# Mixer weights split by DMA on GpSimd's queue, and all convolution taps on VectorE, in a hybrid decoder trunk

## Chip, core and metric

One of the cores of a Trainium2 chip runs the whole program. The metric is the device time of one execution in microseconds (us); the median of three runs of the kernel before is 1012.71 us.

## What is computed

Two layers, each a half-step SwiGLU FFN, a token mixer and a second half-step FFN, all with RMSNorm before and after, on 256 tokens of 1024 channels in float32. The mixer, cut to what matters here:

```python
def hybrid_mixer(h, w_in, ..., w_out):
    p = h @ w_in                      # 1024 x 2064
    gq, gk, gv, gr, glr, ca, cg, sq, sk, sv = jnp.split(p, offsets, axis=-1)
    o_gla  = gla_group(...)           # gated linear attention, 4 heads
    o_conv = conv_group(ca, cg, ...)  # GLU, causal depthwise convolution of width 31, LayerNorm, swish
    o_swa  = swa_group(sq, sk, sv, swa_sinks)   # sliding-window attention, 8 query heads
    return jnp.concatenate([o_gla, o_conv, o_swa], axis=-1) @ w_out   # 1024 x 1024
```

## The kernel before

**Tiling.** The 256 tokens are two tiles of 128 (t = 0 and 1). Every large product is made of three matmuls (`mm3`, lines 178 to 181): activations and weights are each split into a rounded part (`hi`, type float32r) and the rest (`lo`), and hi·hi, hi·lo and lo·hi are added up in PSUM.

**The weight stream.** All weights come as units, in the order of use, through `emit_unit` (line 148). A unit is up to 512 KB: 128 partitions by 1024 floats. A unit of kind "f" belongs to an FFN, one of kind "m" to a mixer. For every unit SyncE's queue (SP) issues a load into one of four `raw` buffers (line 155), ScalarE (ACT) rounds it into `hi` (line 159), and VectorE (DVE) subtracts to get `lo` (line 165); in a mixer 10 of the 28 units take GpSimd (POOL) for that subtraction. There are eight `hi` and eight `lo` buffers, called slots here. A unit takes the slot of the unit eight before it, when TensorE (PE) has read that one for the last time. The raw load needs only a raw buffer, so it runs ahead of the slot.

**The mixer's units.** In this text m0 to m27 are the units of one mixer. The input projection has five groups of columns in the order c, k, q, b, a (line 116), with four units each: m0 to m3 (c), m4 to m7 (k, half as wide), m8 to m11 (q), m12 to m15 (b), m16 to m19 (a). m20 to m27 are the output projection. `c0` is group c for tile 0. The order in which the mixer's pieces are written stands in `SCRIPT` (line 120): c0 k0 c1 T016 k1 q0 S00 S01 ... where T016 is 16 convolution taps, S the attention scores, O attention outputs, G, K, L and P the linear attention, Y the LayerNorm, W the output projection. The framework then orders the instructions of each engine, and each engine takes its own queue in that order; an instruction that waits holds all behind it on its engine, DMA issues included.

**Between FFN and mixer.** `post` (line 276) adds the FFN's output to x and `pre` (line 253) makes the normalized, transposed input of the mixer, for each tile. Both need `rstd`, a power on POOL (line 243): four of them at the start of a mixer, for post and pre of tiles 0 and 1.

**Convolution.** 31 taps for two halves of the channels (c = 0, 1). For c = 0 DVE multiplies and adds (line 636); for c = 1 ACT multiplies (line 639) and POOL adds (line 640). Tap 0 of both is ACT's.

Of the kernel before, what the change touches and what calls it, by code (L numbers as in the profile page):

```python
# [7 lines left out]
F32 = mybir.dt.float32  # L8
# [3 lines left out]
AF = mybir.ActivationFunctionType  # L12
ALU = mybir.AluOpType
# [3 lines left out]
P = 128  # L17
# [25 lines left out]
def trunk_kernel(  # L43
# [6 lines left out]
    V, G, A, PE = nc.vector, nc.gpsimd, nc.scalar, nc.tensor  # L50

    cp = ctx.enter_context(tc.tile_pool(name="cp", bufs=1))
    wp = ctx.enter_context(tc.tile_pool(name="wp", bufs=1))
# [7 lines left out]
    def nm(s):  # L61
        uid[0] += 1
        return f"{s}_{uid[0]}"
# [1 line left out]
    def ps_tile(tag):  # L65
        return pa.tile([P, 512], F32, tag=tag, name=nm(tag), bufs=2)

# [1 line left out]
    A.preload_act_table_set("silu_and_others")  # L69
    xs = []  # L70
    for t in range(T):
# [7 lines left out]
    A.dma_start(out=grow, in_=norm_g.rearrange("l n (k p) -> (l n k) p", p=P))  # L79
    ident = cst[:, C_ID:C_ID + P]  # L80

# [1 line left out]
    units = []  # L83

    DSPLIT = 2
# [57 lines left out]
    NB = 8  # L143
    RAW = 4
    split = {}
    state = {"emitted": 0, "released": 0, "m": 0}

    def emit_unit(i):
        src, nk, w, kind = units[i]
        raw = wp.tile([P, 1024], F32, tag="raw", name=nm("raw"), bufs=RAW)  # L150
        hi = wp.tile([P, 1024], F32R, tag="hi", name=nm("hi"), bufs=NB)
        lo = wp.tile([P, 1024], F32R, tag="lo", name=nm("lo"), bufs=NB)
        n = nk * w
        rv = raw[:, :n].rearrange("p (k n) -> p k n", k=nk)
        nc.sync.dma_start(out=rv, in_=src)
        if i == 1:
            for t in range(1, T):
                nc.sync.dma_start(out=xs[t], in_=x_d[t * P:(t + 1) * P, :])
        A.copy(out=hi[:, :n], in_=raw[:, :n])  # L159
        eng = V  # L160
        if kind == "m":
            state["m"] += 1
            if (state["m"] - 1) % 28 >= 8 and state["m"] % 2 != 0:
                eng = G
        eng.tensor_tensor(out=lo[:, :n], in0=raw[:, :n], in1=hi[:, :n].bitcast(F32), op=ALU.subtract)  # L165
        split[i] = (hi[:, :n].rearrange("p (k n) -> p k n", k=nk),
                    lo[:, :n].rearrange("p (k n) -> p k n", k=nk))

    def top_up():
        while state["emitted"] < len(units) and state["emitted"] - state["released"] < NB:  # L170
            emit_unit(state["emitted"])
            state["emitted"] += 1
# [62 lines left out]
        nc.sync.dma_start(out=g, in_=norm_g[l, n].partition_broadcast(P))  # L235
        return g

# [1 line left out]
    def rstd_of(ss, m=1.0):  # L239
        r = sp.tile([P, 1], F32, tag="rstd", name=nm("rstd"), bufs=8)  # L240
        v = sp.tile([P, 1], F32, tag="var", name=nm("var"), bufs=2)
        V.tensor_scalar(out=v, in0=ss[:, 0:1], scalar1=ss[:, 1:2], scalar2=m * RMS_EPS, op0=ALU.add, op1=ALU.add)  # L242
        G.tensor_tensor(out=r, in0=v, in1=mhalf[:, 0:1], op=ALU.pow)  # L243
        return r
# [39 lines left out]
            xh = xs[t][:, h * 512:(h + 1) * 512]  # L284
            V.scalar_tensor_tensor(out=xh, in0=ys[h], scalar=r, in1=xh, op0=ALU.mult, op1=ALU.add)

# [1 line left out]
    def ffn(first, xT, after, setup=None):  # L288
        acc = [[None, None] for _ in range(T)]
        for t in range(T):  # L290
# [104 lines left out]
                x0 = after(t, acc[t])  # L395
        return [x0, lambda: after(1, acc[1])]

# [1 line left out]
    def sigm(out, in_, scale):  # L399
        A.activation(out=out, in_=in_, func=AF.Exp, scale=scale)  # L400
        A.activation(out=out, in_=out, func=AF.Ln, bias=one)
        A.activation(out=out, in_=out, func=AF.Exp, scale=-1.0)

    def mixer(l, first, xT, after):
        with tc.issue_after(state["silu"].ins):
            ld = A.preload_act_table_set("natural_log_exp_and_others")
        with tc.issue_after(ld.ins):
            return mixer_body(l, first, xT, after)

    def mixer_body(l, first, xT, after):  # L410
# [39 lines left out]
        def tmp(ring, w=256, parts=P):  # L450
            r = mp.tile([P, 256], F32, tag=f"t{ring}", name=nm(f"t{ring}"), bufs={"c": 3, "g": 5, "s": 3}[ring])
            return r[:parts, :w]
# [3 lines left out]
        glr = [mp.tile([P, 16], F32, tag=f"glr{t}", name=nm("glr")) for t in range(T)]  # L456
        qk = [mp.tile([P, 256], F32, tag=f"qk{t}", name=nm("qk")) for t in range(T)]

        # convolution: GLU
        def conv_in(t, ps):  # L460
            sg = tmp("c")
            sigm(sg, ps[:, 256:512], nr[t])
            u = tmp("c")
            V.scalar_tensor_tensor(out=u, in0=ps[:, 0:256], scalar=xT[t][2], in1=sg, op0=ALU.mult, op1=ALU.mult)
            pt = ps_tile("tr")
            for c in range(2):
                PE.transpose(out=pt[:, c * P:(c + 1) * P], in_=u[:, c * P:(c + 1) * P], identity=ident)
            o0 = TAPS - 1 + t * P
            A.copy(out=upad[:, :, o0:o0 + P], in_=pt[:, :256].rearrange("p (c n) -> p c n", c=2))
# [15 lines left out]
            A.activation(out=qk[t], in_=ps[:, 0:256], func=AF.Copy, scale=r)  # L485
            A.activation(out=v_[t][:, 0:136], in_=ps[:, 256:392], func=AF.Copy, scale=r)

        # GLA: log gates, their sums inside a chunk, decayed keys and queries
        kx = mp.tile([P, 2, P], F32, tag="kx", name=nm("kx"))

        REG = []
# [130 lines left out]
            V.tensor_tensor(out=og, in0=og, in1=gr[t], op=ALU.mult)  # L622
            return og

        # convolution: taps, LayerNorm, swish
        yt = sp.tile([P, 512], F32, tag="junk", name=nm("cy"), bufs=1)
        y = [yt[:, 0:S], yt[:, S:2 * S]]
        taps = []

        def tap(c, k):  # L630
            w = cwT[:, l, c, :]
            yc, uk = y[c], upad[:, c, k:k + S]
            if k == 0:
                A.activation(out=yc, in_=uk, func=AF.Identity, scale=w[:, 0:1], bias=w[:, TAPS:TAPS + 1])
            elif c == 0:
                V.scalar_tensor_tensor(out=yc, in0=uk, scalar=w[:, k:k + 1], in1=yc, op0=ALU.mult, op1=ALU.add)  # L636
            else:
                m = tmp("c")
                A.activation(out=m, in_=uk, func=AF.Copy, scale=w[:, k:k + 1])  # L639
                G.tensor_tensor(out=yc, in0=m, in1=yc, op=ALU.add)  # L640

        for k in range(TAPS):
            for c in range(2):
                taps.append(lambda c=c, k=k: tap(c, k))
# [24 lines left out]
            V.tensor_tensor(out=yn, in0=yn, in1=sy, op=ALU.mult)  # L669
            return yn  # L670

        # sliding-window attention
        sv = [mp.tile([P, P], F32, tag=f"sv{t}", name=nm("sv")) for t in range(T)]

        def kv_in(t, ps):
# [88 lines left out]
        scs, qps, gates, qs, ats, ogs, yns = {}, {}, {}, {}, {}, {}, {}  # L764
# [43 lines left out]
            run(op)  # L808
        return [x0[0], lambda: after(1, accs[1])]

# [1 line left out]
    late = []  # L812
    xT = [pre(0, 0, 0), lambda: pre(1, 0, 0)]
    top_up()
# [70 lines left out]
```

## Time and profile before

| | us |
|---|---|
| runs | 1016.26, 1011.55, 1012.71 (median 1012.71) |
| span of the profiled execution | 1010.4 |
| PE busy | 967.4 (96% of the span) |
| DVE busy | 620.7 (61%) |
| ACT busy | 544.3 (54%) |
| POOL busy | 138.8 (14%) |
| DMA, mean over the span | 169 GB/s, 171.26 MB |

The median lies 2.3 us above the span of the profiled execution; this is what lies around the instructions, and the spread of runs (4.7 us). The two mixers take some 128 us each, from about 196 to 324 us and from about 700 to 832 us; the rest is FFN. A profile's slices show PE full in the FFNs; in the mixers the busy shares of DVE and POOL rise and that of PE falls. Busy time of PE is that of pipelined matmuls, so the start times of successive matmuls are used below rather than their durations.

### The profile page before, as it was taken

What the parts mean: (1) busy time and instruction counts of PE and PEld (TensorE: products, weight loads), DVE (VectorE), ACT (ScalarE), POOL (GpSimd) and SP (SyncE); (2) the same over time, 40 slices, a digit from 0 to 9 for tenths busy, and PEclk for the clock granted to TensorE, in tenths of its full rate; (3) what the DMA queues carried; (4) which work ended last, traced back from release to release, by engine and by line L of the source; (5) the groups of instructions that cost most, each with busy time, mean ns of one, the idle gap of its engine ahead of it and who ended that gap; (6) DMA issues with size and microseconds to landing.
All of it is one profiled execution on the core that took longest, in us unless ns stands there. A gap on an engine that the chain in (4) does not pass through costs nothing.

```text
span 1010.4 us, 13066 instructions
## 1 busy us (share of the span) xinstructions
PE 967.4 (96%) x4721; PEld 823.0 (81%) x4721; DVE 620.7 (61%) x948; ACT 544.3 (54%) x927; POOL 138.8 (14%) x154
## 2 busy tenths in 40 slices
PE   7999999997889999999999999999878999999997
PEld 7788888876678988888898888898666898888896
DVE  6555455569898755454576455456698885555453
ACT  7534444577775744444475444356877585444441
POOL 1120000037541000000000000001675210000000
PEclk9999999999999999999999999999989999999999
DMA  8756655553233766655567666464422348666541
GB/s 284 263 178 197 187 167 179 147 186 119 77 89 121 242 200 198 187 171 169 151 197 253 191 182 193 148 224 144 129 84 85 96 157 268 190 186 194 158 148 42
DMA packets 81953, 171.26 MB, mean 169 GB/s; under 512 B 6178, under 2 KB 29920, under 8 KB 81889
## 3 DMA queue, kind: packets, MB, share of 16 engines
q1 hardware_dynamic: 79952, 168.97, 53.8%
q10 hardware_dynamic: 1937, 1.45, 0.8%
q8 instruction: 37, 0.61, 0.2%
q14 instruction: 27, 0.22, 0.1%
HBM read 169.36 MB, written 1.05 MB: 169 GB/s over the span
## 4 chain that ended last, share of the span: by engine, by line
PE 82%; DVE 9%; DMA 3%; ACT 3%; issue 2%; POOL 1%; SPq 0%; POOLq 0%; DVEq 0%; ACTq 0%
PE gu L180 17%; PE gu L179 17%; PE gu L181 17%; PE ga L179 4%; PE ga L180 4%; PE ga L181 4%; PE sa L181 4%; PE sa L179 4%; PE sa L180 4%; DVE cy L636 3%; PE tr L319 2%; DVE E L520 1%; DVE lo L165 1%; PE sa L709 1%; PE tr L262 1%
## 5 line engine op out<-in xcount | busy, mean ns | idle before, releaser
L165 DVE TENSOR_TENSOR lo<-raw,hi 128x1024 fp32r<-128x1024 f32 (+3 forms) x316 | 370.2, 1177 | 317.3 <-ACT hi L159 316.8
L159 ACT CAST hi<-raw 128x1024 fp32r<-128x1024 f32 (+2 forms) x336 | 332.1, 995 | 363.8 <-PE gu L181 218.8
L179 PE MATMUL gu<-hi,xh 128*128 128x512 f32 (+2 forms) x864 | 326.2, 378 | 0.9 <-ACT xh L266 0.9
L180 PE MATMUL gu<-lo,xh 128*128 128x512 f32 (+2 forms) x864 | 325.3, 376 | 0.0
L181 PE MATMUL gu<-hi,xl 128*128 128x512 f32 (+2 forms) x864 | 325.0, 376 | 0.0
L181 PEld LDWEIGHTS gu<-hi,xl 128*128 128x128 f32 x864 | 163.6, 189 | 23.0
L180 PEld LDWEIGHTS gu<-lo,xh 128*128 128x128 f32 x864 | 163.8, 190 | 22.6 <-DVE lo L165 0.4
L179 PEld LDWEIGHTS gu<-hi,xh 128*128 128x128 f32 x864 | 163.5, 189 | 23.0 <-ACT xh L266 1.3
L243 POOL TENSOR_TENSOR rstd<-var,mhalf 128x1 f32<-128x1 f32 x24 | 13.2, 549 | 732.2 <-DVE var L242 732.2
L181 PE MATMUL sa<-hi,hl 128*128 128x512 f32 x176 | 69.0, 392 | 0.0
L179 PE MATMUL ga<-hi,hh 128*128 128x512 f32 x176 | 68.8, 391 | 0.0
L179 PE MATMUL sa<-hi,hh 128*128 128x512 f32 x176 | 68.8, 391 | 0.0
L181 PE MATMUL ga<-hi,hl 128*128 128x512 f32 x176 | 68.6, 390 | 0.0
L180 PE MATMUL ga<-lo,hh 128*128 128x512 f32 x176 | 68.6, 390 | 0.0
L180 PE MATMUL sa<-lo,hh 128*128 128x512 f32 x176 | 68.5, 389 | 0.0
L165 POOL TENSOR_TENSOR lo<-raw,hi 128x1024 fp32r<-128x1024 f32 (+1 forms) x20 | 49.0, 2457 | 31.2 <-ACT hi L159 31.2
L640 POOL TENSOR_TENSOR cy<-tc,cy 128x256 f32<-128x256 f32 x60 | 48.4, 806 | 31.4 <-ACT tc L639 27.8
L636 DVE SCALAR_TENSOR_TENSOR cy<-upad,cwT,cy 128x256 f32<-128x256 f32 x60 | 43.6, 726 | 1.3
L181 PEld LDWEIGHTS ga<-hi,hl 128*128 128x128 f32 x176 | 33.0, 188 | 6.9
L180 PEld LDWEIGHTS sa<-lo,hh 128*128 128x128 f32 x176 | 33.1, 188 | 6.9
L181 PEld LDWEIGHTS sa<-hi,hl 128*128 128x128 f32 x176 | 33.0, 188 | 6.8
L179 PEld LDWEIGHTS sa<-hi,hh 128*128 128x128 f32 x176 | 33.0, 188 | 6.8
(182 smaller groups left out, 1009.9 us busy)
## 6 DMA issues: line engine op xcount, KB each, us to landing
raw<-in_ffn_w_down_dram SPq DMA_DIRECT2D x88, 512.0 KB, 3.4
raw<-in_ffn_w_gate_dram SPq DMA_DIRECT2D x64, 512.0 KB, 3.8
raw<-in_ffn_w_up_dram SPq DMA_DIRECT2D x64, 512.0 KB, 3.8
raw<-in_ffn_w_gate_dram SPq DMA_DIRECT2D x32, 384.0 KB, 3.3
raw<-in_ffn_w_up_dram SPq DMA_DIRECT2D x32, 384.0 KB, 3.4
raw<-in_w_in_dram SPq DMA_DIRECT2D x16, 512.0 KB, 5.5
raw<-in_w_out_dram SPq DMA_DIRECT2D x16, 512.0 KB, 3.4
raw<-in_w_in_dram SPq DMA_DIRECT2D x16, 392.0 KB, 3.7
```

The costliest lines, as they stand in the source:

```text
L159: A.copy(out=hi[:, :n], in_=raw[:, :n])
L165: eng.tensor_tensor(out=lo[:, :n], in0=raw[:, :n], in1=hi[:, :n].bitcast(F32), op=ALU.subtract)
L179: PE.matmul(out=out, lhsT=xh, rhs=wh, start=start, stop=False)
L180: PE.matmul(out=out, lhsT=xh, rhs=wl, start=False, stop=False)
L181: PE.matmul(out=out, lhsT=xl, rhs=wh, start=False, stop=stop)
L243: G.tensor_tensor(out=r, in0=v, in1=mhalf[:, 0:1], op=ALU.pow)
L262: PE.transpose(out=ps[:, i * P:(i + 1) * P], in_=x[:, k * P:(k + 1) * P], identity=ident)
L319: PE.transpose(out=ps[:, i * P:(i + 1) * P], in_=h[:, i * P:(i + 1) * P], identity=ident)
L520: V.tensor_tensor(out=E[:, o:o + P // 4 * R].rearrange("p (c n) -> p c n", n=n), in0=bv[:, :, n - 1:n].to_broadcast([P, P // (4 * s_), n]) ...
L636: V.scalar_tensor_tensor(out=yc, in0=uk, scalar=w[:, k:k + 1], in1=yc, op0=ALU.mult, op1=ALU.add)
L640: G.tensor_tensor(out=yc, in0=m, in1=yc, op=ALU.add)
L709: PE.matmul(out=pqv, lhsT=qp[:, g * 2 + pi, :], rhs=kbd[:, g, :, 0:W], start=True, stop=True)
```

## The change

For units of kind "m" there is no raw buffer and no load on SP any more. GpSimd's queue issues a DMA from the weights straight into `hi`, which converts float32 to float32r; ACT writes `lo` = -`hi`; then GpSimd's queue issues a second DMA that reads the same weights again and adds them into `lo`. No subtraction is left for a mixer's units on DVE or POOL. In the convolution the taps of c = 1 go to DVE as well, so ACT's multiplications and POOL's additions are gone.

```diff
 def emit_unit(i):
     src, nk, w, kind = units[i]
-    raw = wp.tile([P, 1024], F32, tag="raw", name=nm("raw"), bufs=RAW)
     hi = wp.tile(...)
     lo = wp.tile(...)
     n = nk * w
+    split[i] = (hi view, lo view)
+    if kind == "m":
+        G.dma_start(out=split[i][0], in_=src)
+        A.activation(out=lo[:, :n], in_=hi[:, :n].bitcast(F32), func=AF.Copy, scale=-1.0)
+        G.dma_start(out=split[i][1], in_=src, accum_op=ALU.add)
+        return
+    raw = wp.tile([P, 1024], F32, tag="raw", name=nm("raw"), bufs=RAW)
...
     A.copy(out=hi[:, :n], in_=raw[:, :n])
-    eng = V
-    if kind == "m":
-        state["m"] += 1
-        if (state["m"] - 1) % 28 >= 8 and state["m"] % 2 != 0:
-            eng = G
-    eng.tensor_tensor(out=lo[:, :n], in0=raw[:, :n], in1=hi[:, :n].bitcast(F32), op=ALU.subtract)
+    V.tensor_tensor(out=lo[:, :n], in0=raw[:, :n], in1=hi[:, :n].bitcast(F32), op=ALU.subtract)
...
     if k == 0:
         A.activation(out=yc, in_=uk, func=AF.Identity, scale=w[:, 0:1], bias=w[:, TAPS:TAPS + 1])
-    elif c == 0:
+    else:
         V.scalar_tensor_tensor(out=yc, in0=uk, scalar=w[:, k:k + 1], in1=yc, op0=ALU.mult, op1=ALU.add)
-    else:
-        m = tmp("c")
-        A.activation(out=m, in_=uk, func=AF.Copy, scale=w[:, k:k + 1])
-        G.tensor_tensor(out=yc, in0=m, in1=yc, op=ALU.add)
```

The order on the engines moves with it. In the next two fences stands POOL's queue where the first mixer begins: L243 is the power for `rstd`, in the order post and pre of tile 0, post and pre of tile 1, and L421 a small step for pre's. Before:

```order
L243 TENSOR_TENSOR rstd_1664<-var_1665,mhalf 128x1
L243 TENSOR_TENSOR rstd_1679<-var_1680,mhalf 128x1
L421 TENSOR_SCALAR nr_1794<-rstd_1679 128x1
L243 TENSOR_TENSOR rstd_1846<-var_1847,mhalf 128x1
L243 TENSOR_TENSOR rstd_1861<-var_1862,mhalf 128x1
L421 TENSOR_SCALAR nr_1907<-rstd_1861 128x1
L165 TENSOR_TENSOR lo_1961<-raw_1959,hi_1960 128x1024
```

And of the change, in two pieces (hi_1567, hi_1584 and hi_1605 are m0 to m2; between the pieces stand the issues for the `hi` of m3 and m4, the power for pre of tile 0 and its L421; hi_1762, hi_1767 and hi_1772 are m5 to m7, and lo_1735, lo_1740, lo_1763, lo_1768 and lo_1773 the `lo` of m3 to m7):

```order
L156 DMA hi_1567<-in_w_in_dram 128x2x512
L156 DMA hi_1584<-in_w_in_dram 128x2x512
L158 DMA lo_1568<-in_w_in_dram 128x2x512
L156 DMA hi_1605<-in_w_in_dram 128x2x512
L158 DMA lo_1585<-in_w_in_dram 128x2x512
L158 DMA lo_1606<-in_w_in_dram 128x2x512
L243 TENSOR_TENSOR rstd_1661<-var_1662,mhalf 128x1
```

```order
L156 DMA hi_1762<-in_w_in_dram 128x2x256
L158 DMA lo_1735<-in_w_in_dram 128x2x512
L158 DMA lo_1740<-in_w_in_dram 128x2x256
L156 DMA hi_1767<-in_w_in_dram 128x2x256
L158 DMA lo_1763<-in_w_in_dram 128x2x256
L156 DMA hi_1772<-in_w_in_dram 128x2x256
L243 TENSOR_TENSOR rstd_1838<-var_1839,mhalf 128x1
L158 DMA lo_1768<-in_w_in_dram 128x2x256
L243 TENSOR_TENSOR rstd_1853<-var_1854,mhalf 128x1
L421 TENSOR_SCALAR nr_1899<-rstd_1853 128x1
L158 DMA lo_1773<-in_w_in_dram 128x2x256
```

Before, no other instruction stood between the powers; now the first stands behind the three DMA pairs of m0 to m2, and the last two stand between the pairs of m3 to m7.

The second place is DVE's queue where the convolution's taps (L636) meet the first attention scores (L713 before, L709 in the change). Before:

```order
L464 SCALAR_TENSOR_TENSOR tc_1913<-gu_1816,rstd_1679,tc_1909 128x256
L165 TENSOR_TENSOR lo_1973<-raw_1971,hi_1972 128x1024
L165 TENSOR_TENSOR lo_1997<-raw_1995,hi_1996 128x1024
L165 TENSOR_TENSOR lo_2062<-raw_2060,hi_2061 128x784
L464 SCALAR_TENSOR_TENSOR tc_2005<-gu_1952,rstd_1861,tc_2001 128x256
L165 TENSOR_TENSOR lo_2086<-raw_2084,hi_2085 128x784
L636 SCALAR_TENSOR_TENSOR cy_1813<-upad,cwT,cy_1813 128x256 x13
L713 ISA sc_2132,mx_2133<-sa_2134,alibi,snk 128x128
```

And of the change:

```order
L270 SCALAR_TENSOR_TENSOR xl_1872<-tr_1886,gT,xh_1864 128x128
L464 SCALAR_TENSOR_TENSOR tc_1905<-gu_1808,rstd_1676,tc_1901 128x256
L464 SCALAR_TENSOR_TENSOR tc_1993<-gu_1944,rstd_1853,tc_1989 128x256
L636 SCALAR_TENSOR_TENSOR cy_1805<-upad,cwT,cy_1805 128x256 x33
L709 ISA sc_2102,mx_2103<-sa_2104,alibi,snk 128x128
```

The four subtractions of mixer units are gone from there, and 33 taps instead of 13 stand ahead of the first scores.

## Rows read from the trace of the kernel before

**Rows 1.** Busy time by engine, whole span: us, share, instructions
```profile
PE 967.4 (96%) x4721; PEld 823.0 (81%) x4721; DVE 620.7 (61%) x948; ACT 544.3 (54%) x927; POOL 138.8 (14%) x154
```

**Rows 2.** Busy time by stretch: both mixers, then a part of the first
```profile
core 0: us, PE busy (x) PEld busy (x) DVE busy (x) ACT busy (x) POOL busy (x), PEclk, DMA share, GB/s
196.00:324.00 128.00, 114.48 (x605) 94.15 (x604) 105.63 (x244) 91.96 (x228) 60.22 (x62) 0.97 0.34 109
700.00:832.00 132.00, 117.70 (x635) 99.60 (x634) 107.40 (x246) 94.51 (x228) 59.51 (x61) 0.96 0.37 120
244.00:300.00 56.00, 50.03 (x267) 41.09 (x265) 50.56 (x137) 43.00 (x114) 30.84 (x33) 0.95 0.27 86
```

**Rows 3.** Timeline of PE, first mixer: start, us, what, [idle before, releaser]
```profile
203.73 0.39 PE L179 MATMUL gu<-hi,xh 128*128 128x512 f32 x1
203.96 0.39 PE L180 MATMUL gu<-lo,xh 128*128 128x512 f32 x1
...
221.70 0.28 PE L181 MATMUL ga<-hi,xl 128*128 128x256 f32 x1
...
241.70 0.67 PE L709 MATMUL sa<-kbd,qp 128*128 128x256 f32 x2 [3.55 <-DVE mx L713]
...
244.04 0.63 PE L181 MATMUL gu<-hi,xl 128*128 128x512 f32 x1
```

**Rows 4.** Busy time by stretch, around the stall at 241.70
```profile
237.90:241.70 3.80, 0.25 (x2) 0.03 (x1) 3.73 (x8) 1.81 (x4) 3.74 (x3) 1.00 0.01 2
241.70:246.40 4.70, 4.70 (x15) 4.16 (x16) 4.70 (x18) 1.99 (x9) 3.91 (x4) 0.64 0.68 218
```

**Rows 5.** Groups of DVE by line, 196 to 324 us: xcount, busy us, mean ns
```profile
L636 DVE SCALAR_TENSOR_TENSOR cy<-upad,cwT,cy 128x256 f32<-128x256 f32 x30 | 22.1, 735 | 0.7
L165 DVE TENSOR_TENSOR lo<-raw,hi 128x1024 fp32r<-128x1024 f32 x7 | 11.9, 1700 | 5.3 <-ACT hi L159 5.3
L165 DVE TENSOR_TENSOR lo<-raw,hi 128x784 fp32r<-128x784 f32 x4 | 4.9, 1221 | 3.2 <-ACT hi L159 3.2
L165 DVE TENSOR_TENSOR lo<-raw,hi 128x512 fp32r<-128x512 f32 x4 | 2.5, 684 | 0.0
```

**Rows 6.** Timeline of DVE: taps beside POOL's additions, and one with POOL idle
```profile
228.79 12.22 DVE L636 SCALAR_TENSOR_TENSOR cy<-upad,cwT,cy 128x256 f32<-128x256 f32 x13
...
246.22 0.48 DVE L636 SCALAR_TENSOR_TENSOR cy<-upad,cwT,cy 128x256 f32<-128x256 f32 x1
```

**Rows 7.** Timeline of ACT: roundings of m0 to m3, sums of squares
```profile
183.57 1.05 ACT L159 CAST hi<-raw 128x1024 fp32r<-128x1024 f32 x1 [1.03 <-PE gu L181]
...
188.43 1.05 ACT L159 CAST hi<-raw 128x1024 fp32r<-128x1024 f32 x1 [0.94 <-PE sa L181]
...
195.97 0.60 ACT L250 ACTIVATE junk<-ga 128x512 f32<-128x512 f32 x1 [1.41 <-PE ga L181]
...
197.27 1.06 ACT L159 CAST hi<-raw 128x1024 fp32r<-128x1024 f32 x1 [0.61 <-PE sa L181]
```

**Rows 8.** Timeline of POOL: powers of post, tiles 0 and 1
```profile
196.99 0.57 POOL L243 TENSOR_TENSOR rstd<-var,mhalf 128x1 f32<-128x1 f32 x1 [140.36 <-DVE var L242]
...
205.72 0.57 POOL L243 TENSOR_TENSOR rstd<-var,mhalf 128x1 f32<-128x1 f32 x1 [4.38 <-DVE var L242]
```

**Rows 9.** DMA issues: KB each, median us from issue to landing
```profile
raw<-in_w_in_dram SPq DMA_DIRECT2D x16, 512.0 KB, 5.5
raw<-in_w_out_dram SPq DMA_DIRECT2D x16, 512.0 KB, 3.4
```

**Rows 10.** Groups of POOL and ACT by line, 196 to 324 us
```profile
L640 POOL TENSOR_TENSOR cy<-tc,cy 128x256 f32<-128x256 f32 x30 | 24.3, 809 | 15.5 <-ACT tc L639 13.7
L165 POOL TENSOR_TENSOR lo<-raw,hi 128x1024 fp32r<-128x1024 f32 (+1 forms) x10 | 24.5, 2454 | 15.2 <-ACT hi L159 15.1
L639 ACT ACTIVATE tc<-upad,cwT 128x256 f32<-128x256 f32 x30 | 14.1, 505 | 1.8 <-POOL cy L640 1.6
```

More of the change, by code (lines that the diff above doesn't have):

```diff
@@ L145, in trunk_kernel @@
     split = {}
-    state = {"emitted": 0, "released": 0, "m": 0}
+    state = {"emitted": 0, "released": 0}
     def emit_unit(i):
         src, nk, w, kind = units[i]
-        raw = wp.tile([P, 1024], F32, tag="raw", name=nm("raw"), bufs=RAW)
         hi = wp.tile([P, 1024], F32R, tag="hi", name=nm("hi"), bufs=NB)
@@ L153, in emit_unit @@
         n = nk * w
+        split[i] = (hi[:, :n].rearrange("p (k n) -> p k n", k=nk),
+                    lo[:, :n].rearrange("p (k n) -> p k n", k=nk))
+        if kind == "m":
[4 more added lines that the diff above has]
+        raw = wp.tile([P, 1024], F32, tag="raw", name=nm("raw"), bufs=RAW)
         rv = raw[:, :n].rearrange("p (k n) -> p k n", k=nk)
@@ L159, in emit_unit @@
         A.copy(out=hi[:, :n], in_=raw[:, :n])
-        eng = V
-        if kind == "m":
-            state["m"] += 1
-            if (state["m"] - 1) % 28 >= 8 and state["m"] % 2 != 0:
-                eng = G
-        eng.tensor_tensor(out=lo[:, :n], in0=raw[:, :n], in1=hi[:, :n].bitcast(F32), op=ALU.subtract)
-        split[i] = (hi[:, :n].rearrange("p (k n) -> p k n", k=nk),
-                    lo[:, :n].rearrange("p (k n) -> p k n", k=nk))
+        V.tensor_tensor(out=lo[:, :n], in0=raw[:, :n], in1=hi[:, :n].bitcast(F32), op=ALU.subtract)
     def top_up():
```

## The prediction

> **What bounds the kernel now.** I read the shares by engine first, then the two mixers as stretches of their own, then the places in them where PE waits, and last the times at which slots and sums come free.
>
> PE is busy 967.4 of 1010.4 us [rows 1], so what is left to win lies in the 43 us in which it is idle. The two mixers hold 13.5 (128 - 114.48) and 14.3 (132 - 117.70) of these, and in them the granted clock is 0.97 and 0.96 [rows 2], which costs about 3% of 128 and 4% of 132, 3.8 and 5.3 us. So a change that touches the mixers alone can win at most 13.5 + 14.3 + 3.8 + 5.3 = 37 us. From 244 to 300 us the idle time and the clock make 6.0 + 2.5 = 8.5 us, while DVE is busy 50.56 of 56 [rows 2]: there DVE sets the pace. The longest stall is of that kind: at 241.70 PE has waited 3.55 us for the first scores [rows 3], which stand behind 13 taps on DVE. In the stall PE was nearly idle; behind it 4.70 us ran at a mean granted clock of 0.64, below the upper level of 2.4 GHz, before the clock was full again [rows 4]. A stall thus costs about (1 - 0.64) x 4.70 = 1.7 us more than its length. Weights are not what PE waits for there: SP loads them into raw buffers ahead of the slot, and a slot that comes free needs only ACT's 1.05 us [rows 7] and the subtraction.
>
> **What the change takes off the engines.** In the first mixer DVE loses 11.9 + 4.9 + 2.5 = 19.3 us of subtractions [rows 5]. It gains 30 taps. A tap takes 0.48 us with POOL idle, but 13 of them took 12.22 us beside POOL's additions, 0.94 each [rows 6]; with these gone I price all 60 at 0.48, 28.8 us against 22.1 now [rows 5], +6.7. DVE is relieved by 12.6 us a mixer. POOL loses 24.3 + 24.5 us of work, ACT 14.1 us of multiplications [rows 10]; neither bounds the mixer, so I cost both at nothing. ACT's rounding of a unit becomes a negation of the same size. The second reading of the weights adds 2 x 28 units, some 25 MB; the DMA share in a mixer is 0.34 to 0.37 [rows 2], so bandwidth covers that and I cost it at nothing; were the queue full, it would show in the landing time below.
>
> **What it adds: two landings in a row.** The raw load ran ahead of the slot. The first DMA now writes the slot itself, so it can't be issued before PE has let go of it; then come a landing, 1.05 us of ACT and a second landing. No DMA of POOL's queue and none that adds is in the trace. The nearest rows are the unit loads on SP, 3.4 us from issue to landing for the output projection and 5.5 for the input projection [rows 9]. I take 5.5 for both, since it is the load of the same matrix at the same place, and keep 3.4 for both as the lower end and 11 for the adding one (twice 5.5, since it reads two things) as the upper. For POOL's time to issue I take 0.5 us.
>
> By 5.5 us the page "DMA: Bandwidth & Descriptors" of the Trainium skill disagrees: its fit for this path ("Anatomy of one DMA") is 2.0 us plus the bytes by 436 GB/s, so 3.2 us for 524288 bytes, an estimate by that page, and no run here shows it. By that figure the sum would be that of the rival below that wins.
>
> **Step by step, first mixer.** m0's slot is free at 183.5, m2's at 188.4 [rows 7]. In POOL's queue m2's first issue stands behind m0's second, which waits for landing (189.0) and ACT (190.1): m2 lands at 196.1 and is negated by 197.2. ACT's sums of squares for post of tile 0 stand behind that negation; the last half began at 195.97 [rows 7], now both run from 197.2 to 198.4. The power, 196.99 before [rows 8], starts at 198.7: +1.7 us for all that follows.
>
> m3's slot is free at 197.3 [rows 7]. Its first issue is behind that power, 199.3; landed 204.8, second issue 205.9, landed 211.4. Group c starts at 203.73 + 1.7 = 205.4 and has used m0 to m2 by 209.2 (a matmul each 0.23 us [rows 3]): PE waits 2.2 us. m5 to m7 get their slots at 204.1 to 205.4. POOL's queue now takes turns, and each second issue waits for the landing before it: m5 at 204.1 and 210.3, m6 at 207.6 and 213.8, m7 at 210.8 and 217. m7 is whole at 222.5. The power for post of tile 1, 205.72 before [rows 8], comes at 211.3, +5.6, and that for pre at 215.5; both are early enough for c1, which stands behind m7. Behind it come five half-wide matmuls of k0 (half of 0.23 each, 0.6), 19 of c1 (4.4) and 24 half-wide ones of k1 (2.8), so with 1.7 for the slow clock k1 ends at about 222.5 + 0.6 + 4.4 + 2.8 + 1.7 = 232.0, against 222.0 [rows 3]: PE loses about 10 us.
>
> Group q goes into the slots that c1 lets go, from 221.5 to about 229. By the same count its last unit lands at 246.2, and q1 ends at 248.5 instead of 244.4 [rows 3]: only 4.1 us later, since PE was waiting for DVE in that stretch. Meanwhile DVE does its 33 taps, 33 x 0.48 = 15.8 us, from about 231 to 247: the taps are off the path. The first three units of b keep PE until about 252; m15 is whole at 255.7 (3.7 us of waiting), and m16, which follows 1.1 us of b0, at 259.9 (3.1 us). Attention's scores fill some of these 6.8 us; I take 5.5. So a0 is 4.1 + 5.5 = 9.6 us late.
>
> **The sum.** Per mixer: 9.6 us until a0, plus 1.7 for the slow clock behind the last of these waits, less what DVE's relief wins back. Of the 8.5 us between 244 and 300 I give back half, 4.2, because those stalls are also waits on attention's own chain. That is +7.1 a mixer, +14.2 for both: 1010.4 + 14.2 = 1024.6 for the span, and with the 2.3 us by which the median stands above it **1027 us**. What the FFNs do is unchanged.
>
> **Rivals.**
>
> *The relief decides (faster).* If both DMAs land in 3.4 us, each of the eight landings in a row on the way to a0 is 2.1 us shorter, 17 us, more than the 9.6: weights no longer bind, DVE's 12.6 us relief is on the path, and the whole 8.5 us is won in each mixer, 1012.7 - 17 = 996. It decides once a landing costs about 4.3 us or less (9.6 / 8 = 1.2 less than 5.5). For it speaks the 3.4 of the output projection and DVE's share; against it the 5.5 at the very place, and the powers behind DMAs.
>
> *The adding DMA is slow.* At 11 us its five landings in a row (m2, m7, m11, m19 and the output projection's last) add 5 x 5.5 = 27.5 us a mixer: 1027 + 55 = 1082. For it: it reads, adds and writes; against it: nothing in the trace.
>
> *DVE holds POOL's DMAs up.* The taps were slowed from 0.48 to 0.94 us beside POOL [rows 6], so the two engines do get in each other's way. If a run of 33 taps kept POOL from issuing, m11's first issue, due at about 234, would wait until 247, 12.6 us in each mixer: 1027 + 25 = 1052. The page "SBUF — State Buffer" of the Trainium skill ("SBUF: two separate sides") has such a rule: GpSimd can't write descriptors while VectorE runs in a two-port mode. It names copies, casts and `tensor_scalar` for that, and infers that two SBUF inputs alone don't do it, so by that page the taps would not.
>
> *No difference.* The waits for weights and the relief cancel: 1012.7. For it: q1 loses only 4.1 of the 10 us.
>
> That the conversion doesn't round would change `lo`, not the time.
>
> **How the numbers follow.** Chances: the forecast's case (about 1015 to 1045) 0.46, relief 0.22, slow adding DMA 0.16, held up 0.06, no difference 0.10. The likeliest is the forecast, so 1027 stands. Its own range is 1015 to 1045. To leave out no more than 2 in 10 the range goes down to the relief's 996 and up into the slow case, where 7.5 us for the adding DMA instead of 11 gives 1027 + 2 x 5 x 2 = 1047 and 10 us 1072: 996 to 1072. A measurement of this kernel tells 0.5%, 5 us, from no change. Faster by more than that: 0.23 (relief, and a little of no difference); within it 0.11; slower 0.66.
>
> **What would show it.** Right: in the first 30 us of each mixer PE waits for `lo` and `hi` of m3, m7 and m11; the power for post of tile 1 starts some 5 us later after the FFN's last matmul; taps take 0.48 us; the stretch from the first scores to the mixer's end is shorter than now. Wrong: PE waits that stay with DVE (then landings are short and it is faster), second issues that land more than 8 us after they go out, or gaps between POOL's issues just while DVE's taps run.

## The result, and the profile after

The changed kernel takes **1062.47 us** (1059.25 to 1065.36, 4 runs) against 1013.23 (1011.55 to 1016.26) for the kernel before on the same chip: ratio 1.0482, 95% interval 1.0462 to 1.0502. That is 49 us slower. The forecast was 14 us slower, so the sign was right and the size far off: 1062 lies above the forecast's own range, 1015 to 1045, and inside the wide one, 996 to 1072, only by the case of the slow adding DMA. The FFNs did not change; each mixer lost some 24.7 us.

The page's busy times and DMA queues, after [rows 1 for before]:

```profile
PE 988.1 (93%) x4721; PEld 838.2 (79%) x4721; DVE 567.5 (54%) x972; ACT 518.2 (49%) x867; POOL 144.5 (14%) x186
...
q1 hardware_dynamic: 66768, 143.67, 44.2%
q0 software_dynamic: 26368, 50.60, 22.8%
```

PE does the same 4721 matmuls and is "busy" 20.7 us longer with them, which is the lower clock of the next view. q0 is GpSimd's DMA queue; it takes 0.45% of the DMA engines per MB, SP's q1 0.31%.

The first mixer by stretch. Before, 196 to 324 us held 605 matmuls [rows 2]; after, 605 matmuls need 196 to 348 us:

```profile
core 0: us, PE busy (x) PEld busy (x) DVE busy (x) ACT busy (x) POOL busy (x), PEclk, DMA share, GB/s
196.00:348.00 152.00, 124.70 (x605) 102.91 (x604) 82.26 (x261) 80.62 (x200) 57.97 (x73) 0.89 0.81 175
226.00:236.00 10.00, 7.16 (x29) 6.19 (x30) 2.55 (x9) 4.33 (x15) 2.57 (x4) 0.66 0.51 79
276.00:286.00 10.00, 7.94 (x33) 7.05 (x31) 3.37 (x9) 2.95 (x7) 2.15 (x2) 0.55 0.94 166
```

This gives the books of the mixer. PE's idle time went from 128 - 114.48 = 13.5 to 152 - 124.70 = 27.3 us, +13.8. The same matmuls took 124.70 instead of 114.48 us, +10.2: the mean granted clock fell from 0.97 to 0.89, and in the two stretches shown, each behind a wait for weights, it came near its lower level, 1.2 GHz of 2.4 (0.66 and 0.55). Together +24.0. The DMA share is 0.81, not 0.34, at only 175 GB/s. (This share counts the time that packets took. It passes 1 in views below, so it does not say how full the engines are.)

What PE waits for there, by releaser: total us, times, longest:

```profile
PE gu L180 <- DMA lo<-in_w_in_dram: 9.4, 5, 3.8
PE ga L180 <- DMA lo<-in_w_in_dram: 6.6, 3, 3.3
PE tr L262 <- DVE x L285: 5.9, 1, 5.9
PE sa L679 <- ACT ts L674: 2.2, 1, 2.2
...
PE gu L180 <- DMA lo<-in_w_out_dram: 0.4, 1, 0.4
```

Waits for `lo` are 9.4 + 6.6 + 0.4 = 16.4 us. The 5.9 for x is the late power of post. Six of the eight waits for `lo` of the input projection lie in groups c, k and q; the other two are for group b and for group a:

```profile
275.37 0.70 PE L180 MATMUL ga<-lo,xh 128*128 128x392 f32 x1 [2.75 <-DMA lo<-in_w_in_dram]
...
279.43 0.66 PE L180 MATMUL gu<-lo,xh 128*128 128x392 f32 x1 [2.06 <-DMA lo<-in_w_in_dram]
```

That leaves 27.3 - 22.3 = 5.0 us for everything else, where before all 13.5 were of that kind.

The timelines of ACT and POOL where the mixer begins [rows 7 and 8 for before]: start, us, what, [idle before, releaser]. ACT:

```profile
191.18 1.06 ACT L157 ACTIVATE lo<-hi 128x1024 fp32r<-128x1024 f32 x1 [7.51 <-DMA hi<-in_w_in_dram]
...
201.33 1.06 ACT L157 ACTIVATE lo<-hi 128x1024 fp32r<-128x1024 f32 x1 [7.38 <-DMA hi<-in_w_in_dram]
202.29 0.58 ACT L250 ACTIVATE junk<-ga 128x512 f32<-128x512 f32 x1
```

And POOL:

```profile
193.31 1.24 POOL L156 DMA_DIRECT2D hi<-in_w_in_dram  x1
...
204.02 0.57 POOL L243 TENSOR_TENSOR rstd<-var,mhalf 128x1 f32<-128x1 f32 x1
...
217.53 1.10 POOL L243 TENSOR_TENSOR rstd<-var,mhalf 128x1 f32<-128x1 f32 x1
224.15 1.22 POOL L158 DMA_DIRECT2D lo<-in_w_in_dram  x1 [5.52 <-ACT lo L157]
225.78 0.56 POOL L243 TENSOR_TENSOR rstd<-var,mhalf 128x1 f32<-128x1 f32 x1 [0.41 <-DVE var L242]
...
226.90 1.26 POOL L158 DMA_DIRECT2D lo<-in_w_in_dram  x1 [0.24 <-ACT xh L266]
```

ACT stands 7.38 us for m2's `hi`, with the sums of squares queued behind its negation; the power starts at 204.02 instead of 196.99. m7's second issue goes out at 226.90.

Landings, in the stretch 180 to 350 us: KB each, median us from issue to landing [rows 9 for before]:

```profile
hi<-in_w_in_dram POOLq DMA_DIRECT2D x8, 512.0 KB, 5.8
lo<-in_w_in_dram POOLq DMA_DIRECT2D x8, 512.0 KB, 6.9
...
hi<-in_w_in_dram POOLq DMA_DIRECT2D x8, 392.0 KB, 9.4
lo<-in_w_in_dram POOLq DMA_DIRECT2D x8, 392.0 KB, 7.3
hi<-in_w_in_dram POOLq DMA_DIRECT2D x4, 256.0 KB, 6.2
lo<-in_w_in_dram POOLq DMA_DIRECT2D x4, 256.0 KB, 6.5
```

And VectorE's taps, as a group (count, busy us, mean ns) [rows 5], and the 33 ahead of the first scores on the timeline:

```profile
L636 DVE SCALAR_TENSOR_TENSOR cy<-upad,cwT,cy 128x256 f32<-128x256 f32 x60 | 24.9, 479 | 4.0 <-ACT cy L634 3.9
...
246.11 13.29 DVE L636 SCALAR_TENSOR_TENSOR cy<-upad,cwT,cy 128x256 f32<-128x256 f32 x33 [3.92 <-ACT cy L634]
```

A tap takes 0.479 us, as predicted. In a row they take less, 13.29 / 33 = 0.40 us each, since one starts before the other has ended: the 60 taps keep VectorE busy for 24.9 us, where the forecast had 28.8.

### The profile page after: what moved, and what is told of

The parts are those of the page before. It is cut to its first block, busy times and chain, and to the rows that moved or that the text cites. A ratio compares the mean times of both kernels' runs of the same rounds, so it can differ in the third digit from the quotient of the medians.

```text
span 1059.8 us, 12996 instructions
## 1 busy us (share of the span) xinstructions
PE 988.1 (93%) x4721; PEld 838.2 (79%) x4721; DVE 567.5 (54%) x972; ACT 518.2 (49%) x867; POOL 144.5 (14%) x186
## 4 chain that ended last, share of the span: by engine, by line
PE 71%; DMA 11%; issue 8%; POOL 4%; ACT 3%; DVE 2%; POOLq 0%; SPq 0%; DVEq 0%; ACTq 0%
PE gu L180 15%; PE gu L181 15%; PE gu L179 15%; DMA hi<-in_w_in_dram 4%; PE ga L181 4%; PE ga L179 4%; PE ga L180 3%; PE sa L181 3%; PE sa L180 3%; PE sa L179 3%; DMA hi<-in_w_out_dram 2%; DMA lo<-in_w_in_dram 2%; PE tr L319 2%; POOL lo L158 1%; DMA raw<-in_ffn_w_gate_dram 1%
## 5 line engine op out<-in xcount | busy, mean ns | idle before, releaser
L167 DVE TENSOR_TENSOR lo<-raw,hi 128x1024 fp32r<-128x1024 f32 (+1 forms) x280 | 324.1, 1163 | 298.1 <-ACT hi L166 297.7
L166 ACT CAST hi<-raw 128x1024 fp32r<-128x1024 f32 (+1 forms) x280 | 280.7, 1007 | 339.0 <-PE gu L181 211.7
L180 PE MATMUL gu<-lo,xh 128*128 128x512 f32 (+2 forms) x864 | 330.0, 382 | 20.3 <-DMA lo<-in_w_in_dram 20.1
L181 PE MATMUL gu<-hi,xl 128*128 128x512 f32 (+2 forms) x864 | 329.3, 381 | 0.0
L180 PEld LDWEIGHTS gu<-lo,xh 128*128 128x128 f32 x864 | 166.8, 193 | 48.4 <-issue 12.9
L157 ACT ACTIVATE lo<-hi 128x1024 fp32r<-128x1024 f32 (+2 forms) x56 | 52.3, 939 | 88.8 <-DMA hi<-in_w_in_dram 69.9
L156 POOL DMA_DIRECT2D hi<-in_w_in_dram x40 | 38.6, 1260 | 316.9 <-DVE lo L167 288.7
L243 POOL TENSOR_TENSOR rstd<-var,mhalf 128x1 f32<-128x1 f32 x24 | 14.2, 594 | 401.5 <-DVE var L242 401.4
L158 POOL DMA_DIRECT2D lo<-in_w_in_dram x40 | 49.7, 1380 | 76.3 <-ACT lo L157 65.7
L636 DVE SCALAR_TENSOR_TENSOR cy<-upad,cwT,cy 128x256 f32<-128x256 f32 x120 | 49.8, 480 | 7.6 <-ACT cy L634 7.6
```

The source lines that it names most:

```text
L156: G.dma_start(out=split[i][0], in_=src)
L157: A.activation(out=lo[:, :n], in_=hi[:, :n].bitcast(F32), func=AF.Copy, scale=-1.0)
L158: G.dma_start(out=split[i][1], in_=src, accum_op=ALU.add)
L167: V.tensor_tensor(out=lo[:, :n], in0=raw[:, :n], in1=hi[:, :n].bitcast(F32), op=ALU.subtract)
L180: PE.matmul(out=out, lhsT=xh, rhs=wl, start=False, stop=False)
L181: PE.matmul(out=out, lhsT=xl, rhs=wh, start=False, stop=stop)
```

## The experiments

All times are medians; the kernel before ran 1013.9 to 1014.5 us beside them. Edits are to the changed kernel unless said otherwise.

**e2_weights: the weights' part alone.** The convolution is put back:

```diff
+    elif c == 0:
+        V.scalar_tensor_tensor(...)
+    else: A.activation(...); G.tensor_tensor(out=yc, in0=m, in1=yc, op=ALU.add)
```

> The other part alone: mixer weights by the two DMAs on GpSimd's queue, taps of c = 1 on ScalarE and GpSimd as before. A and B: at least as slow as the change, 1060 to 1085 us, since GpSimd's additions now stand between its DMA issues and slow the taps down. If the taps are a loss (C): under 1055 us.

Measured: 1070.44, ratio 1.0554 (1.0515 to 1.0593). The weights cost 56 us, as expected, and moving the taps on top of that wins some 7 to 8 back (56 less 49, or 1070.4 less 1062.5), about 4 a mixer.

**e1_taps: the taps' part alone**, as an edit of the kernel before.

```diff
-    elif c == 0:
+    else:
         V.scalar_tensor_tensor(...)
-    else: A.activation(...); G.tensor_tensor(...)
```

> The kernel before with one part of the change alone: all convolution taps on VectorE; the weights are loaded and split as before. Theory A (two landings in a row behind every slot) and theory B (the adding DMA fills the DMA engines) both put the whole loss on the weights, so this is no slower than before: 1003 to 1014 us. VectorE's 60 taps a mixer take 0.40 us each as in the profile of the change (24 us in place of 22), and what POOL's additions did to its neighbours goes. Rival C (the taps on VectorE are themselves a loss): over 1018 us.

Measured: 1021.26, ratio 1.0057 (1.0034 to 1.0079): a loss of about 6 us, as rival C had it and not as expected. So the same move lost here and won on top of the new weights. I read that as the work of DVE and POOL beside it: with 19.3 us of subtractions still on DVE and POOL's beside it, a tap takes 0.54 us and VectorE is busy 103.9 of 128 us in the first mixer, about as before [rows 2].

**e3_plain2: the second DMA writes instead of adding.** Same order, same waits; `lo` is then the weights themselves.

```diff
-    G.dma_start(out=split[i][1], in_=src, accum_op=ALU.add)
+    G.dma_start(out=split[i][1], in_=src)
```

> The change with the second DMA writing instead of adding (its output is then not the split: lo holds the weights a second time, the subtraction is left out). Order and waits stay. A: the landings stay at 6 to 7 us and the time within 8 us of the change's 1062 us. B: landings of lo fall to 3 to 5 us and the time to 1045 us or less.

Measured: 1024.98, ratio 1.009 (1.0068 to 1.0113). Adding instead of writing costs 1062.5 - 1025.0 = 37.5 us, as theory B had it. In the same stretch the landings are shorter by 2 us for the very DMA that changed, and by 0.8 for the other one:

```profile
hi<-in_w_in_dram POOLq DMA_DIRECT2D x8, 512.0 KB, 5.0
lo<-in_w_in_dram POOLq DMA_DIRECT2D x8, 512.0 KB, 4.9
```

**e4_nochain: and no negation, so the two DMAs go out side by side.**

```diff
-    A.activation(out=lo, in_=hi, func=AF.Copy, scale=-1.0)
-    G.dma_start(out=split[i][1], in_=src, accum_op=ALU.add)
+    G.dma_start(out=split[i][1], in_=src)
```

> As the run before, and ScalarE's negation is left out too, so that the second DMA waits for the slot alone and goes out beside the first (same bytes, same number of DMAs, no adding, no subtraction). A: one landing in place of two and of ScalarE's step, about 7 to 8 us less at each of the four rounds of slots in a mixer: 1015 to 1035 us. B or bandwidth alone: both DMAs still compete, 1045 to 1060 us.

Measured: **982.76**, ratio 0.9683 (0.9657 to 0.9708). The series of landing, negation and landing costs 42.2 us more; expected were 1015 or above. With the weights in time and the split left out, the kernel is 31 us faster than before. Its first mixer, and its densest 20 us:

```profile
196.00:324.00 128.00, 126.11 (x695) 107.12 (x694) 93.73 (x282) 71.75 (x197) 48.09 (x74) 1.00 0.75 217
226.00:246.00 20.00, 20.00 (x107) 16.84 (x106) 19.22 (x66) 8.18 (x30) 9.00 (x13) 1.00 1.42 382
```

The same bytes flow at 382 GB/s there and PE never waits. So reading the weights twice is not what costs; what counts is how, and in what order.

**e5_actwait: as e4_nochain, but ACT still waits for every first landing.**

```diff
-    A.activation(out=lo, in_=hi, func=AF.Copy, scale=-1.0)
-    G.dma_start(out=split[i][1], in_=src, accum_op=ALU.add)
+    A.activation(out=scr, in_=hi[:, :128], func=AF.Copy, scale=-1.0)
+    G.dma_start(out=split[i][1], in_=src)
```

> The two DMAs of a mixer unit go out beside each other and both only write, as in e4_nochain (982.8 us), but ACT again waits in its queue for the first landing of every unit: it reads 128 columns of hi and writes a scrap that nobody uses. Leaves out the subtraction that makes lo. This splits the 42 us between e4_nochain and e3_plain2 (1025.0). Theory Q (queue: what costs is ACT standing still for a landing, with its sums of squares, GLU and softmax steps behind it): 1010 to 1025, first power at about 200 to 201 as in e3_plain2. Theory S (series: what costs is that the second landing starts after the first, and that POOL's issues wait for it): 982 to 995, first power at 198 to 200.

Measured: 993.92, ratio 0.9815 (0.9785 to 0.9844), first power at 198.57: on theory S's side. Of the 42.2 us, ACT's standing is 11.2; the other 31.0 come with the second DMA waiting for the first. That part holds three things which no run separates: the second landing itself, POOL's later issues queued behind a second issue that waits, and ACT's full negation (0.94 us in the mean) in place of the scrap (0.31).

**e6_addnochain: adding, without the series.**

```diff
-    A.activation(out=lo, in_=hi, func=AF.Copy, scale=-1.0)
+    A.activation(out=lo, in_=xs[0], func=AF.Copy, scale=0.0)
```

> The second DMA adds again, but into a lo that ACT has filled with zeros (zero times x of tile 0) as soon as the slot is free, so it need not wait for the first landing. Leaves out the subtraction that makes lo. This prices the adding alone, without the series. Theory T (throughput: adding costs DMA and POOL issue time, 37 us wherever it stands): 1015 to 1030. Theory L (latency: adding costs through its longer landing, which two landings in a row make visible): 983 to 1000, although the landings of lo stay at 6 to 9 us.

Measured: 1008.24, ratio 0.9944 (0.9923 to 0.9964), between the two expectations. Without the series adding still costs up to 25.5 us over e4_nochain (ACT's 56 fills and the wait of the second issue for them are in that); in the series it costs 37.5. So it is more than a longer latency, and the price depends on where it stands: landings of 512 KB rise to 8.7 (`hi`) and 10.4 us (`lo`), and packets take longer for the same bytes (a DMA share of 1.11 at 255 GB/s, against 1.42 at 382 in e4_nochain):

```profile
226.00:296.00 70.00, 63.23 (x340) 52.05 (x340) 49.45 (x176) 45.96 (x110) 39.87 (x49) 0.98 1.11 255
```

**e9_probe: the price by itself.** The kernel before, and behind its end DMAs of 512 KB on POOL's queue with the other engines idle but for ACT's eight negations ahead of the adding ones.

```diff
+    plain(hs[0:1]); plain(hs)          # 1, then 8 that write
+    add(ls[0:1]); add(ls)              # 1, then 8 that add
+    G.dma_start(out=ls[0], in_=r_, accum_op=ALU.add); G.dma_start(out=hs[0], in_=r_)
```

> The kernel before, and behind its end a row of DMAs from the weights into free buffers, 512 KB each, on GpSimd's queue, with every engine idle: one that only writes (casting to float32r), eight of these in a row, one that adds, eight that add, one that adds from SBUF, one that writes from SBUF. Its whole time says nothing; the landings are read. Theory T (an adding DMA is dearer for the DMA engines themselves): eight plain land in 11 to 14 us at 300 to 380 GB/s, eight adding in 16 to 22 us; alone, 3.5 to 5 against 5 to 7 us. Rival (they are alike, and only what else runs in a mixer makes the adding ones late): the two rows within 10% of each other.

POOL's timeline: rows L856 (write) and L861 (add) are the issues, and each L851 starts when one more DMA has landed:

```profile
1022.20 5.79 POOL L856 DMA_DIRECT2D ph<-in_w_in_dram  x8 [0.21 <-issue]
...
1030.41 0.21 POOL L851 TENSOR_SCALAR probe<-ph 128x1 f32<-128x1 f32 x1 [1.87 <-DMA ph<-in_w_in_dram]
...
1037.13 0.21 POOL L851 TENSOR_SCALAR probe<-ph 128x1 f32<-128x1 f32 x1 [1.09 <-DMA ph<-in_w_in_dram]
...
1046.71 9.86 POOL L861 DMA_DIRECT2D pl<-in_w_in_dram  x8 [0.20 <-issue]
...
1058.49 0.21 POOL L851 TENSOR_SCALAR probe<-pl 128x1 f32<-128x1 f32 x1 [1.35 <-DMA pl<-in_w_in_dram]
...
1071.21 0.21 POOL L851 TENSOR_SCALAR probe<-pl 128x1 f32<-128x1 f32 x1 [2.33 <-DMA pl<-in_w_in_dram]
```

Eight that write are in after 14.9 us, eight that add after 24.5, both somewhat later than expected; in a row one more lands every (1037.13 - 1030.41) / 5 = 1.34 us against (1071.21 - 1058.49) / 5 = 2.54, which is 1.90 times. Issues take 5.79 / 8 = 0.72 us against 9.86 / 8 = 1.23. One alone lands in 4.1 us when it writes and 6.4 when it adds; from SBUF instead of DRAM 2.9 and 4.6. So theory T holds, in this one run: the two rows are far more than 10% apart with nothing else in flight.

The page "Collectives: The Full Stack" of the Trainium skill ("The bandwidth ceiling: the fold count and why AG ≠ RS ≠ AR") explains with an add why reduce-scatter runs at about half the rate of all-gather, measured there as 1.93: the add needs two source reads, which go through the same ring, and a copy one. The 1.90 here is near that figure; that the reason is the same for this DMA, no run here shows.

**e7_defer: the head of the mixer unblocked.** m2's negation and second DMA are ordered behind post's sums of squares on ACT and its power on POOL.

```diff
+    with tc.issue_after(state["sq"].ins), tc.issue_after(state["pow"].ins):
+        rest()      # negation and adding DMA of m2
```

> The changed kernel, with the negation and second DMA of m2 moved behind the sums of squares of post of tile 0 on ACT and behind that power on POOL; all else as in the change. Theory Q (the head start is lost because sums of squares and power stand behind landings): first power back at 197.0 to 199, c0 some 5 us earlier, and the time 1062 less 5 to 16 us, 1046 to 1057. Theory S (units bind): c0 moves by less than 2 us, since m2 or m3 is then as late as before, and the time stays within 1058 to 1065.

Measured: 1060.0, ratio 1.0457 (1.0428 to 1.0485). The power came to 200.11, 3.9 us earlier, not all the way; in place of the 5.9 us wait for x, PE now waits for m2 and its followers:

```profile
210.95 0.50 PE L185 MATMUL gu<-lo,xh 128*128 128x512 f32 x1 [0.98 <-DMA lo<-in_w_in_dram]
217.20 0.77 PE L185 MATMUL gu<-lo,xh 128*128 128x512 f32 x1 [4.59 <-DMA lo<-in_w_in_dram]
226.82 0.55 PE L185 MATMUL ga<-lo,xh 128*128 128x256 f32 x1 [2.96 <-DMA lo<-in_w_in_dram]
```

The blocked power was real, but removing it is worth 2 to 3 us at most, and the two intervals overlap: the weights were as late.

**e8_rawadd: one landing instead of two, the adding kept.** Raw loads and roundings as before; the adding DMA takes `raw` from SBUF.

```diff
+    A.copy(out=hi, in_=raw)
     A.activation(out=lo, in_=hi, func=AF.Copy, scale=-1.0)
-    G.dma_start(out=split[i][1], in_=src, accum_op=ALU.add)
+    G.dma_start(out=lo[:, :n], in_=raw[:, :n], accum_op=ALU.add)
```

> Raw loads ahead of the slot on SP and ACT's rounding as in the kernel before; then ACT writes lo = -hi, and the adding DMA takes raw from SBUF instead of the weights from DRAM. So one landing after the slot instead of two, with the adding kept; all taps on VectorE. Theory S and L (what costs is two landings in a row): 1000 to 1030. Theory T (the adding costs wherever it stands): 1035 to 1060.

Measured: 1030.51, ratio 1.0175 (1.014 to 1.021), half a us above the first range. Taking one of the two landings away, and with it half of the DMAs on POOL's queue, returns 32 of the 49 us; one adding landing of 5.7 us behind every slot is still more than the relief is worth.

**e16_chainlate: where it is paid.** m0 to m11 (groups c, k, q) as in the kernel before, m12 to m27 with the two DMAs, taps on VectorE.

```diff
     if kind == "m":
+      if j >= 12:      # j: the unit's number in its mixer
         G.dma_start(...); A.activation(...); G.dma_start(..., accum_op=ALU.add)
         return
```

> The changed kernel (two DMAs per unit, taps all on VectorE), but m0 to m11 (groups c, k and q) get their weights as in the kernel before; m12 to m27 stay with the two DMAs. Tells where the 50 us are paid. Theory E (early: PE needs m0 to m11 soon after their slots come free, groups b, a and the output projection have slack): 1010 to 1028. Rival (everywhere: every unit pays its share, 16 of 28 units with 0.56 of the bytes): 1038 to 1050.

Measured: 1011.52, ratio 0.9987 (0.9966 to 1.0007). With the first twelve units as before, the loss of 49 us is gone. In the first mixer PE waits for no weights at all; its longest waits are others:

```profile
PE sa L700 <- ACT sq L697: 6.4, 2, 3.9
PE sa L750 <- ACT pT L743: 1.2, 1, 1.2
```

But the late units are not free. The longest of these waits, 3.9 us before 233.82, is for a step of attention on ACT (1.9 us in the kernel before) that stands behind the negations of late units, and these had waited for landings:

```profile
227.37 0.87 ACT L161 ACTIVATE lo<-hi 128x784 fp32r<-128x784 f32 x1 [1.99 <-DMA hi<-in_w_in_dram]
229.96 1.82 ACT L161 ACTIVATE lo<-hi 128x784 fp32r<-128x784 f32 x2 [1.73 <-DMA hi<-in_w_in_dram]
...
233.07 0.69 ACT L697 ACTIVATE sq<-gu,rstd 128x512 f32<-128x512 f32 x1
```

What the sixteen late units cost and what the relief wins just cancel in this run; it does not tell the two apart.

**e10_some and e11_sometaps: ten scattered units.** The kernel before, with m9, m11, ... m27 by ACT's negation and an adding DMA from raw, no subtraction on POOL; e10_some has all taps on VectorE.

```diff
-    if (state["m"] - 1) % 28 >= 8 and state["m"] % 2 != 0: eng = G
+    if j >= 8 and j % 2 == 1: A.activation(...); G.dma_start(out=lo, in_=raw, accum_op=ALU.add)
```

> Raw loads, roundings and VectorE's subtractions as in the kernel before, all taps on VectorE; only the ten units of a mixer that would go to POOL (here m9, m11, ... m27) get lo by ACT's negation and an adding DMA from raw. So POOL does no large work in a mixer. Theory (POOL's work is what slows DVE, and ten adding DMAs with one landing, on units that are read late in their groups, stay hidden): 985 to 1005. Rival (a landing behind the slot is paid wherever it stands, as in e8_rawadd, by 10 of 28): 1010 to 1025.

> As e10_some, but the taps as in the kernel before (c = 1 on ACT and POOL). Theory (POOL's subtractions, not its taps, are what slows DVE): 995 to 1008. Rival (taps beside POOL's additions stay slow and ACT's ten negations come on top): 1010 to 1025.

Measured: 1023.93, ratio 1.0094 (1.0074 to 1.0115), and 1015.59, ratio 1.001 (0.9996 to 1.0024). Both miss the theory's range and lie in the rival's. m9 and m11 are early units, and in e10_some PE stands for their `lo` (0.6 and 1.2 us at 225 and 230 us). Its longest such wait is for a unit of group a, though, a late one:

```profile
253.58 0.45 PE L184 MATMUL gu<-lo,xh 128*128 128x392 f32 x1 [3.04 <-DMA lo<-raw]
```

The group's two negations began only at 245.81 and 247.12, behind softmax steps on ACT, and their DMAs went out at 246.94 and 248.27. So a unit that is read late can still be late when a step of its chain stands behind other work.

**e12_late and e15_latetaps: late units only.** As e11_sometaps and e10_some, with m12 to m27 and no others by adding DMA (m8 and m10 on POOL).

```diff
+    if j >= 12: A.activation(...); G.dma_start(out=lo, in_=raw, accum_op=ALU.add)
+    elif j >= 8 and j % 2 == 0: eng = G
```

> The kernel before, taps as there; m0 to m11 as there; m12 to m27 get lo by ACT's negation and an adding DMA from raw, so POOL subtracts two units only and VectorE ten us less. Theory E (late units have slack, so the relief of DVE and POOL shows): 995 to 1010. Rival (ACT's 16 more negations of 0.8 to 1.05 us, some 15 us, stand before its softmax and GLU steps): 1012 to 1025.

> As e12_late, with all taps on VectorE: ACT loses 14 us of multiplications and POOL 24 us of additions, VectorE gains about 7 us. Theory E: 990 to 1005. Rival (VectorE's taps ahead of the first scores set the pace, as in e1_taps): 1012 to 1022.

Measured: e12_late 1026.45, ratio 1.0123 (1.0105 to 1.0142), slower than either expectation; e15_latetaps **1005.79**, ratio 0.991 (0.9877 to 0.9942), just above theory E's range and 0.9% faster than before. The two differ by the taps alone, 20.7 us. With the taps on ACT and POOL, PE still waits 6.1 us for `lo` from raw in the first mixer, with them on VectorE not at all. I read this as ACT's multiplications and POOL's additions standing between the negations and the DMA issues; it was not tested by itself. The traces bear it out in part: the third negation starts at 233.33 in e12_late, behind multiplications that wait for POOL, and at 228.98 in e15_latetaps; but PE's longest wait for `lo`, 3.15 us before 258.23, follows negations that stood behind softmax steps. First mixer of e15_latetaps, 196 to 324 us:

```profile
196.00:324.00 128.00, 117.58 (x630) 99.71 (x630) 93.84 (x274) 95.86 (x220) 33.25 (x41) 0.97 0.69 176
```

In the 128 us in which the kernel before issued 605 matmuls, 630 go through.

## Why the prediction was wrong, point by point

- **What bounds the mixer** was half right: weights took DVE's place as the bound, as forecast. Waits for m3, m7 and q's units appeared, and the power of post, tile 1, came 11.8 us later (205.72 to 217.53) where 5 had been named.
- **The step that failed is the price of a unit: 5.5 us for both landings and 0.5 us per issue.** The adding DMA was priced by the row of a plain load on SP. It lands in 6.9 us in the median, holds POOL 1.2 to 1.4 us per issue, and in a row it takes 1.9 times as long as one that writes; other DMAs land late beside it: m2's `hi`, between two adding ones, took 7.9 us instead of 5.5. "Bandwidth covers that" failed for the same reason: it counted bytes (e4_nochain shows that they fit), not the time that an adding DMA takes for them. e3_plain2 prices this at 37.5 us. Where both DMAs only write, it lands them in 5.0 and 4.9 us, near the 5.5, and takes 1025.0, 2 us from the forecast; so the price of adding is most of what was missing, though the sum's other terms have errors of both signs, and that closeness is in part luck. The rival "the adding DMA is slow" named the mechanism, but no landing of 11 us stands in a median of the changed kernel: one alone costs 2.3 us more than one that writes, four in a row 4 x 1.2 = 4.8 (e9_probe).
- **The errors add up along the chain.** Power 198.7 forecast, 204.02 measured: ACT's standing behind a landing was priced at 1.7 us, once, and ACT stood 39.2 us in 11 waits for `hi` of the input projection between 180 and 350 us; m7's second issue 217 against 226.90; k1's last matmul 222 before, 232 forecast, 241.2 after; q1's 248.5 against 265.5. Here a second step fell: q was to lose only 4.1 us "since PE was waiting for DVE in that stretch". k1's end slipped past the slack.
- **The slow clock was counted at 1.7 us a mixer** for one wait. It cost 10.2. PE waits for `lo` eight times from group c to group a, and from 196 to 286 us the granted clock was below 0.95 in eight of nine stretches of 10 us.
- **The relief was under-counted, in the other direction.** Waits of PE for things other than weights and the first power fell from 13.5 to 5.0 us, 8.5 won; I gave 4.2. The 4 a mixer between e2_weights and the changed kernel are the taps' part of it. The rest need not be relief: where PE comes late for its weights, the other engines have more time, and no run separates that.
- So the sum was 9.6 + 1.7 - 4.2 = 7.1 a mixer, and what the first mixer shows is 22.3 + 10.2 - 8.5 = 24.0.
- **"The relief decides"** was right in kind: e4_nochain, where weights never bind, is 31 us faster than before, near the 37 us that I gave as the most a change in the mixers can win. Its condition, landings of at most 4.3 us, was not the point: those of e4_nochain take 7.5 us, but not one behind the other.
- **The late units** (5.5 us at b and a) were priced about right for this kernel: 2.75 + 2.06 = 4.8 us. But in e16_chainlate, with c, k and q as before, PE waits for none of them; what they cost there comes by way of ACT.
- **"DVE holds POOL's DMAs up" did not happen.** 33 taps ran from 246.11 to 259.40; in that time POOL issued four DMAs from 245.72 to 249.11 and eight more from 255.15 on; the gap between waited for ACT's negation. The DMA share was 1.08 from 246 to 256 us, so the DMA engines did not stand still either.
- **The rule from "DMA: Bandwidth & Descriptors"** of the Trainium skill ("Anatomy of one DMA"), 3.2 us for 524288 bytes as an estimate, comes near a lone plain DMA: 4.1 us from the issue's start, or 3.4 without the 0.7 of issuing. It does not fit the mixer's 5.8 to 6.9.

Open is how the 31 us of the series split between the second landing, POOL's queue order and ACT's negation.

## What to carry to other kernels

A load that ran ahead of its buffer and becomes a chain behind it (landing, engine, landing) cost this kernel nothing on balance for units that are read late, and 49 us with the units that are read soon: undo it for the first units alone before judging it, and look at what the waiting engine holds up behind it. Price a DMA that adds by its own row, at about twice the DMA time of one that writes, and look at what it does to its neighbours' landings. Count the slow clock behind every stall, not once.

## What the runs showed of the hardware that I had not expected

In e9_probe a DMA that adds into SBUF takes 2.54 us per 512 KB in a row, 206 GB/s, against 1.34 us and 391 GB/s for one that writes; its issue holds GpSimd 1.23 instead of 0.72 us. In e4_nochain two side by side per unit, both writing, ran at 382 GB/s for 20 us beside a full PE without a wait. And the same 30 taps per mixer, moved from ACT and POOL to VectorE, lost 6 us with POOL subtracting beside them (e1_taps), won 7 to 8 with POOL issuing all the units' DMAs, and differed by 21 between e12_late and e15_latetaps.
